# Sixty-four bytes of padding that move the split weight pieces against the token tiles

## The chip, the cores and the metric

One core of a Trainium2 chip. The metric is the device time of the slowest core in microseconds (us); with one core it is that core's. Three runs of the kernel before were timed, and one more execution was recorded by the hardware profiler.

## The reference

Two layers of a hybrid decoder, on 256 tokens of width 1024. In each layer:

```
h = rms_norm(x, ln_w)
q, k, v, g, z, xbc, dt = split(h @ w_in)
attn = moba_attention(rms_norm(q), rms_norm(k), v) * silu(g)
y    = rms_norm(ssd_scan(silu(conv(xbc)), softplus(dt)) * silu(z))
x    = x + concat(attn, y) @ w_out
```

Everything is float32. By far the most arithmetic is in the two projections, `h @ w_in` (1024 by 6672) and the product with `w_out` (2048 by 1024). The scan needs a running sum of `dt * a` over the 256 tokens for each of 16 heads.

## The kernel before

**How a float32 product is made.** The large products are matmuls on the type float32r. A copy into that type rounds, so each operand is split in two: the rounded value, a high piece, and the rest, a low piece. Tokens are split into `hT` and `lT` (in the first stage `hr` and `lr`, in the output projection `ah`/`al` and `sh`/`sl`), weights into `wh` and `wl`. A product is three matmuls: high by high, token low by weight high, token high by weight low.

**How weights come in.** `Weights.pump` (L88) loads pieces of 128 partitions by 2 by 512 floats into one of four `raw` buffers (L76, a DMA issued by SP, L79), makes `wh` from it on ScalarE (L101) and `wl` on VectorE (L102). There are eight `wh` and eight `wl` buffers, of 4096 bytes per partition each, and the pieces are made as far ahead as those allow.

**The two loops that use them.** Both take a weight piece after the other, in the order of the list CHUNKS.

- `mm_tokens` (L212, matmuls at L226 to L228) makes v, q, k and the output projection. The stationary operand is a 128 by 128 block of tokens and the moving one a weight piece, 512 columns wide (348 or 344 for v, and 256 for the last output block).
- `mm_pair` (L233, matmuls at L244 to L246) makes the convolution input, the gates g and z. Here the stationary operand is a 128 by 128 block of a weight piece, and the moving one is 256 tokens.

```
pe.matmul(ps[:, cs], lh[:, kl, tl], wh[:, kk, cs], ...)   # L226, mm_tokens: stationary, moving
pe.matmul(o, wh[:, kk, cs], lh[:, k, :], ...)             # L244, mm_pair: stationary, moving
```

Each matmul brings a weight load of its own (LDWEIGHTS, the engine row PEld), which reads the stationary operand from SBUF while the matmul ahead of it still streams its moving operand.

**What sets the order.** The order of work on TensorE is the order of the program with small tasks (transposes, attention heads, the scan) put in after a set count of steps (`resume`, `tick`). None of it depends on addresses.

**Where the tiles lie.** Pools take SBUF one after the other: `const`, `keep`, `tmp`, `small`, `raw_pool`, `wh_pool`, `wl_pool` (L126 to L132). All token tiles are in `keep`: `hT` begins at byte 38016 of each partition, `lT` at 46208, `ah` at 54400, `al` at 62592, `sh` at 78976, `sl` at 87168. Each of these is 128 more than a multiple of 256. The eight `wh` buffers begin at 162752 and the eight `wl` at 195520, 4096 bytes apart, each 192 more than a multiple of 256, and the `raw` buffers from 146368, 192 more as well. Blocks inside these tiles begin at multiples of 512 bytes. So wherever a token block and a weight piece meet in TensorE, their starts differ by 64 bytes modulo 256: the moving weight is 64 ahead in `mm_tokens`, the moving tokens are 64 behind in `mm_pair`.

`cT` (L417, in `decay`) is a tile of the pool `small`: 16 partitions by 256 floats, 1024 bytes, at byte 144544, with a single buffer. VectorE copies the running sums into it, a DMA stores it to DRAM (L420), and two transposes read it (L427). Behind it in memory come only the last tiles of `small` and then `raw`, `wh` and `wl`, which end at 228288 of 229376 bytes.

Of the kernel before, what the change touches and what calls it, by code (L numbers as in the profile page):

```python
# [9 lines left out]
F32 = mybir.dt.float32  # L10
# [6 lines left out]
S = 256  # L17
# [4 lines left out]
NS = 16  # L22
# [26 lines left out]
class Weights:  # L49
# [38 lines left out]
    def pump(self, upto=None, before=None):  # L88
        nc = self.nc
        upto = len(self.subs) if upto is None else upto  # L90
        while self.prepped < upto and self.prepped - self.freed < NB:
            i = self.prepped
            li, s, wd = self.subs[i]
            self.load(li + RAWB - 1)
            src = self.raw[li]
# [18 lines left out]


RAWB = 4
WARM = 14
URGENT = 400

# [2 lines left out]
def hybrid_kernel(ctx: ExitStack, tc: tile.TileContext, x, par, w, out):  # L122
# [6 lines left out]
    small = ctx.enter_context(tc.tile_pool(name="small", bufs=4))  # L129
    raw_pool = ctx.enter_context(tc.tile_pool(name="raw_pool", bufs=RAWB))  # L130
    wh_pool = ctx.enter_context(tc.tile_pool(name="wh_pool", bufs=NB))
# [5 lines left out]
    def bank(name):  # L137
        return ps_s.tile([P, 512], F32, tag="ps_s", name=name)
# [24 lines left out]

    for i in range(WARM):
        pe.matmul(warm[:, 0:P], ones, ones, start=(i == 0), stop=(i == WARM - 1))

# [223 lines left out]
    def decay(L, dtr, dt, dth, ac, nac, cb):  # L390

        pc = L * NPAR

        def sm_tile(name):
            return small.tile([P, 2, NS], F32, tag=name, name=name, bufs=1)
        ab, e1, zd, z2, pl, da = (sm_tile(n) for n in ("ab", "e1", "zd", "z2", "pl", "da"))
        act.activation(ab, dtr, AF.Abs)
        act.activation(e1, ab, AF.Exp, scale=-1.0)
        dve.tensor_scalar(zd, e1, 2.0, None, ALU.add)
        dve.reciprocal(zd, zd)  # L400
        dve.tensor_tensor(zd, zd, e1, ALU.mult)
        dve.tensor_tensor(z2, zd, zd, ALU.mult)
        dve.tensor_scalar(pl, z2, 1.0 / 17.0, None, ALU.mult)
        for i in range(7, 0, -1):
            dve.scalar_tensor_tensor(pl, pl, 1.0 / (2 * i + 1), z2, ALU.add, ALU.mult)
        dve.scalar_tensor_tensor(pl, pl, 1.0, zd, ALU.add, ALU.mult)
        dve.tensor_scalar(pl, pl, 2.0, None, ALU.mult)
        dve.scalar_tensor_tensor(dt, dtr, 0.0, pl, ALU.max, ALU.add)
        ea = small.tile([P, NS], F32, tag="ea", name="ea", bufs=1)
        act.activation(ea, par_sb[:, pc + C_AL:pc + C_AL + NS], AF.Exp)  # L410
        dve.tensor_tensor(da, dt, ea.unsqueeze(1).to_broadcast([P, 2, NS]), ALU.mult)
        dve.tensor_scalar(dth, dt, 0.5, None, ALU.mult)
        yield 6
        cp = bank("cp")
        pe.matmul(cp[:NS, 0:256], da[:, 0, :], tri[:, 128:384], start=True, stop=False)
        pe.matmul(cp[:NS, 128:256], da[:, 1, :], tri[:, 128:256], start=False, stop=True)
        cT = small.tile([NS, S], F32, tag="cT", name="cT", bufs=1)  # L417
        dve.tensor_copy(cT, cp[:NS, 0:256])
        cd = dram.tile([NS * S], F32, tag="cd", name=f"cd{L}")
        nc.sync.dma_start(cd.rearrange("(h s) -> h s", h=NS), cT)  # L420
        for g in range(NG):
            src = cd[g * 8 * S:(g + 1) * 8 * S].unsqueeze(0).broadcast_to([P, 8 * S])
            nc.sync.dma_start(cb[g].rearrange("p h s -> p (h s)"), src)
        yield 1
        cq = bank("cq")
        for t in range(2):
            pe.transpose(cq[:, t * NS:(t + 1) * NS], cT[:, t * P:(t + 1) * P], ident[:NS, :NS])  # L427
        dve.tensor_copy(ac, cq[:, 0:NS])
        dve.tensor_scalar(nac, cq[:, NS:2 * NS], -1.0, None, ALU.mult)
# [118 lines left out]
    for L in range(NL):  # L548
# [53 lines left out]
        for cs, ts in (((0,), (0, 1)), ((1,), (0, 1)), ((2,), (0, 1))) if L == 0 else (  # L602
# [8 lines left out]
            if L > 0 and ts == (0,):  # L611
                region.__exit__(None, None, None)
        resume(decay(L, dtr, dt, dth, ac, nac, cb))
        qT = keep.tile([P, NH, S], F32, tag="qT", name=f"qT{L}")
        kT = keep.tile([P, NH, S], F32, tag="kT", name=f"kT{L}")
# [153 lines left out]
```

## Time and profile before

| | |
|---|---|
| median of 3 runs | 453.44 us (453.14 to 454.38) |
| profiled execution | 452.3 us |
| its span on the core | 450.5 us |
| TensorE matmul busy | 446.1 us (99%) |
| weight loads busy | 406.0 us (90%) |
| VectorE busy | 346.7 us (77%) |
| ScalarE busy | 279.7 us (62%) |
| granted TensorE clock | 1.00 of 2.4 GHz |

The span is the time from the first to the last instruction of the profiled execution; 1.8 us of its own time lie outside it. Busy time of TensorE counts from a matmul's start to its modelled end, and matmuls overlap; the step from the start of one matmul to the start of the next is what tells how fast TensorE goes.

### The profile page before, as it was taken

Reading aid. Unit: us, or ns where it says so; the run is one execution under the profiler, and the core shown is the slowest. Engines: PE = TensorE matmul, PEld = TensorE weight load, DVE = VectorE, ACT = ScalarE, POOL = GpSimd, SP = SyncE. Lnnn points to the kernel's source line nnn. Section 1 sums busy time; section 2 is a strip of 40 time slices with the busy share of each in tenths; the row PEclk is TensorE's granted clock in tenths of the full one; section 3 lists DMA queues with packets and bytes.
Section 4 is the critical chain, followed back from the end, with each engine's and each line's share of the span. In section 5 each row is a group of like instructions: output and inputs, shape, how many; then the busy total and the mean of one; then the engine's idle time right before and its main releaser. Section 6 shows DMA issues by size and latency. Waiting matters only on the chain.

```text
span 450.5 us, 7880 instructions
## 1 busy us (share of the span) xinstructions
PE 446.1 (99%) x2956; PEld 406.0 (90%) x2956; DVE 346.7 (77%) x636; ACT 279.7 (62%) x571; POOL 23.9 (5%) x29
## 2 busy tenths in 40 slices
PE   9999999999999999999999999999999999999997
PEld 9998878999999999888899878889999989998986
DVE  7597876799999888766565784686999999787621
ACT  7776779778558645534556656977657865555400
POOL 0000320200000000000000011110000000000000
PEclk9999999999999999999999999999999999999999
DMA  8888886452355155556246988561435444553301
GB/s 282 275 250 294 284 302 249 143 185 95 95 188 176 60 160 186 169 188 182 61 138 232 284 278 288 185 227 53 139 109 175 139 141 128 200 180 121 121 25 70
DMA packets 26373, 79.43 MB, mean 176 GB/s; under 512 B 2624, under 2 KB 9440, under 8 KB 25824
## 3 DMA queue, kind: packets, MB, share of 16 engines
q1 hardware_dynamic: 26048, 78.68, 53.3%
q8 instruction: 23, 0.38, 0.3%
q10 hardware_dynamic: 288, 0.27, 0.2%
q14 instruction: 14, 0.11, 0.1%
HBM read 77.85 MB, written 1.08 MB: 175 GB/s over the span
## 4 chain that ended last, share of the span: by engine, by line
PE 99%; DVE 0%; issue 0%
PE o L227 6%; PE o L226 6%; PE o L228 6%; PE xb L244 5%; PE xb L246 5%; PE xb L245 5%; PE z L245 3%; PE v L228 3%; PE z L244 3%; PE v L226 3%; PE v L227 3%; PE z L246 3%; PE k L227 3%; PE g L246 3%; PE g L244 3%; PE g L245 3%
## 5 line engine op out<-in xcount | busy, mean ns | idle before, releaser
L102 DVE TENSOR_TENSOR wl<-raw,wh 128x1024 fp32r<-128x1024 f32 (+3 forms) x145 | 166.0, 1157 | 41.3 <-ACT wh L101 40.1
L101 ACT CAST wh<-raw 128x1024 fp32r<-128x1024 f32 (+3 forms) x145 | 143.9, 999 | 59.8 <-DMA raw<-in_w_dram 15.9
L244 PE MATMUL xb<-hT,wh 128*128 128x256 f32 x192 | 56.3, 293 | 0.0
L245 PE MATMUL xb<-lT,wh 128*128 128x256 f32 x192 | 54.4, 283 | 0.0
L246 PE MATMUL xb<-hT,wl 128*128 128x256 f32 x192 | 53.9, 281 | 0.0
L245 PEld LDWEIGHTS xb<-lT,wh 128*128 128x128 f32 x192 | 36.2, 189 | 0.3
L246 PEld LDWEIGHTS xb<-hT,wl 128*128 128x128 f32 x192 | 36.2, 189 | 0.1
L244 PEld LDWEIGHTS xb<-hT,wh 128*128 128x128 f32 x192 | 36.2, 188 | 0.2
L246 PE MATMUL g<-hT,wl 128*128 128x256 f32 x128 | 36.3, 283 | 0.0
L245 PE MATMUL z<-lT,wh 128*128 128x256 f32 x128 | 36.2, 283 | 0.0
L244 PE MATMUL g<-hT,wh 128*128 128x256 f32 x128 | 36.1, 282 | 0.0
L244 PE MATMUL z<-hT,wh 128*128 128x256 f32 x128 | 36.0, 281 | 0.0
L245 PE MATMUL g<-lT,wh 128*128 128x256 f32 x128 | 35.9, 281 | 0.0
L246 PE MATMUL z<-hT,wl 128*128 128x256 f32 x128 | 35.9, 280 | 0.0
L447 DVE SCALAR_TENSOR_TENSOR cv<-rw,par_sb,cv 128x256 f32<-128x256 f32 x72 | 31.6, 481 | 4.2 <-ACT cv L444 4.2
L226 PE MATMUL k<-wh,hT 128*128 128x512 f32 x64 | 25.4, 397 | 0.0
L227 PE MATMUL k<-wh,lT 128*128 128x512 f32 x64 | 25.4, 397 | 0.0
L228 PE MATMUL k<-wl,hT 128*128 128x512 f32 x64 | 25.4, 397 | 0.0
L227 PE MATMUL q<-wh,lT 128*128 128x512 f32 x64 | 25.1, 394 | 0.0
L226 PE MATMUL q<-wh,hT 128*128 128x512 f32 x64 | 25.1, 394 | 0.0
L227 PE MATMUL o<-wh,al 128*128 128x512 f32 (+1 forms) x64 | 24.7, 386 | 0.0
L228 PE MATMUL q<-wl,hT 128*128 128x512 f32 x64 | 24.6, 395 | 0.0
(197 smaller groups left out, 1106.6 us busy)
## 6 DMA issues: line engine op xcount, KB each, us to landing
raw<-in_w_dram SPq DMA_DIRECT2D x120, 512.0 KB, 4.3
raw<-in_w_dram SPq DMA_DIRECT2D x15, 348.0 KB, 3.7
cb<-cd SPq DMA_DIRECT2D x4, 1024.0 KB, 7.8
raw<-in_w_dram SPq DMA_DIRECT2D x8, 344.0 KB, 3.6
x<-in_x_dram SPq DMA_DIRECT2D x2, 512.0 KB, 5.2
xT<-in_w_dram SPq DMA_DIRECT2D x3, 256.0 KB, 4.3
out_dram<-x SPq DMA_DIRECT2D x3, 256.0 KB, 2.0
raw<-in_w_dram SPq DMA_DIRECT2D x2, 174.0 KB, 3.2
```

Source lines behind the costliest of these rows:

```text
L101: nc.scalar.copy(h[:, ks, :wd], src[:, ks, :wd])
L102: nc.vector.tensor_tensor(lo[:, ks, :wd], src[:, ks, :wd], h[:, ks, :wd].bitcast(F32), ALU.subtract)
L226: pe.matmul(ps[:, cs], lh[:, kl, tl], wh[:, kk, cs], start=first, stop=False)
L227: pe.matmul(ps[:, cs], ll[:, kl, tl], wh[:, kk, cs], start=False, stop=False)
L228: pe.matmul(ps[:, cs], lh[:, kl, tl], wl[:, kk, cs], start=False, stop=final)
L244: pe.matmul(o, wh[:, kk, cs], lh[:, k, :], start=(k == 0 and c == 0), stop=False)
L245: pe.matmul(o, wh[:, kk, cs], ll[:, k, :], start=False, stop=False)
L246: pe.matmul(o, wl[:, kk, cs], lh[:, k, :], start=False, stop=(k == KT - 1 and c == 1))
L447: dve.scalar_tensor_tensor(cv[:, c, :], rw[:, c, k:k + S], cw(k), cv[:, c, :], ALU.mult, ALU.add)
```

## The change

The tile `cT` gets 16 more floats in each partition, and only its first 256 are used. Every tile that lies behind it moves up by 64 bytes: the `raw`, `wh` and `wl` buffers now begin at multiples of 256, and so 128 bytes away from the token tiles, modulo 256, instead of 64. No instruction is added, removed or moved.

```diff
 RAWB = 4
+CT_PAD = 16
 WARM = 14
 URGENT = 400
...
-        cT = small.tile([NS, S], F32, tag="cT", name="cT", bufs=1)
+        cT = small.tile([NS, S + CT_PAD], F32, tag="cT", name="cT", bufs=1)[:, :S]
         dve.tensor_copy(cT, cp[:NS, 0:256])
```

## Rows read from the trace of the kernel before

**Rows 1.** The page: busy time of each engine, then the granted clock by slices.
```profile
PE 446.1 (99%) x2956; PEld 406.0 (90%) x2956; DVE 346.7 (77%) x636; ACT 279.7 (62%) x571; POOL 23.9 (5%) x29
...
PEclk9999999999999999999999999999999999999999
```

**Rows 2.** The page: the chain that ended last, shares of the span by engine.
```profile
PE 99%; DVE 0%; issue 0%
```

**Rows 3.** Waits of the weight loads: who waited for whom, us in total, times, longest.
```profile
PEld warm L165 <- DVE ones L159: 1.1, 1, 1.1
...
PEld cq L427 <- DVE wl L102: 0.7, 2, 0.4
...
PEld q L226 <- ACT wh L101: 0.2, 1, 0.2
```

**Rows 4.** Groups of PE by line and form: operands, count, busy us, mean ns.
```profile
L244 PE MATMUL xb<-hT,wh 128*128 128x256 f32 x192 | 56.3, 293 | 0.0
...
L244 PE MATMUL z<-hT,wh 128*128 128x256 f32 x128 | 36.0, 281 | 0.0
...
L226 PE MATMUL q<-wh,hT 128*128 128x512 f32 x64 | 25.1, 394 | 0.0
...
L226 PE MATMUL o<-wh,ah 128*128 128x512 f32 x56 | 22.1, 395 | 0.0
...
L226 PE MATMUL v<-wh,hT 128*128 128x348 f32 x32 | 10.2, 324 | 0.0
```

**Rows 5.** Timeline of PE, mm_pair: first and last of 50 matmuls, start us.
```profile
153.38 0.28 PE L244 MATMUL g<-hT,wh 128*128 128x256 f32 x1
...
158.93 0.28 PE L245 MATMUL z<-lT,wh 128*128 128x256 f32 x1
```

**Rows 6.** The same later: first and last of 135 matmuls.
```profile
162.09 0.28 PE L246 MATMUL z<-hT,wl 128*128 128x256 f32 x1
...
177.87 0.28 PE L245 MATMUL z<-lT,wh 128*128 128x256 f32 x1
```

**Rows 7.** Timeline of PE, mm_tokens, 512 columns: first and last of 105 matmuls.
```profile
33.10 0.39 PE L226 MATMUL q<-wh,hT 128*128 128x512 f32 x1
...
56.90 0.39 PE L228 MATMUL q<-wl,hT 128*128 128x512 f32 x1
```

**Rows 8.** The same in the second layer: first and last of 62 matmuls.
```profile
252.69 0.40 PE L228 MATMUL q<-wl,hT 128*128 128x512 f32 x1
...
266.92 0.40 PE L226 MATMUL k<-wh,hT 128*128 128x512 f32 x1
```

**Rows 9.** Timeline of PE, mm_tokens, 348 columns: first and last of 71 matmuls.
```profile
8.15 0.32 PE L227 MATMUL v<-wh,lr 128*128 128x348 f32 x1
...
19.35 0.32 PE L226 MATMUL v<-wh,hr 128*128 128x348 f32 x1
```

**Rows 10.** Timeline of PE: seven float32 transposes of 128 columns, two float32 matmuls of 256.
```profile
87.33 0.93 PE L354 MATMUL qtp<-ident,qn 128*128 128x128 f32 x7
...
105.17 0.59 PE L456 MATMUL bp<-bc 128*128 128x256 f32 x2
```

**Rows 11.** Groups of PE by line: the same transposes and matmuls, with their means.
```profile
L354 PE MATMUL qtp<-ident,qn 128*128 128x128 f32 x64 | 8.7, 274 | 0.0
...
L456 PE MATMUL bp<-bc 128*128 128x256 f32 x8 | 2.4, 377 | 0.0
```

**Rows 12.** Timeline of all engines in mm_pair: matmul and weight load side by side.
```profile
153.72 0.28 PE L244 MATMUL g<-hT,wh 128*128 128x256 f32 x1
153.72 0.19 PEld L245 LDWEIGHTS g<-lT,wh 128*128 128x128 f32 x1
```

**Rows 13.** Busy time of VectorE in three windows: window, length, busy us (instructions).
```profile
107.00:120.00 13.00, 13.00 (x27) 1.00 0.48 143
133.00:147.00 14.00, 14.00 (x30) 1.00 0.46 149
325.00:340.00 15.00, 15.00 (x31) 1.00 0.39 125
```

## The prediction

> **What bounds the kernel.** The page first: TensorE's matmuls are busy for 99% of the span, at the full clock (1.00, 2.4 GHz) in every slice [rows 1]. The chain that ended last says the same: 99% of it is PE, none is an engine that PE waited for [rows 2]. The waits of the weight loads name no wait above 1.1 us, and that one is the start of the kernel [rows 3]. So the end is set by TensorE's own pace: by the step from the start of one matmul to the start of the next, times their number.
>
> The groups by form give the numbers [rows 4]. `mm_pair` has (192 + 128 + 128) x 3 = 1344 matmuls of 256 columns (xb, g and z; three lines each). `mm_tokens` has 720 of 512 columns (q and k 64 each, o 56 each of two kinds, three lines each: 192 + 192 + 336), 288 of 348 or 344 (v), and 96 of 256, in all 1104. The mean ns in those rows hold each matmul's run out of the array and overlap, so I read steps from the timeline, as the distance from a first to a last row over their count.
>
> - `mm_pair`: 49 steps in 5.55 us, 113.3 ns [rows 5]; later 134 steps in 15.78 us, 117.8 ns [rows 6].
> - `mm_tokens`, 512 columns: 104 steps in 23.80 us, 228.9 ns [rows 7]; later 61 in 14.23 us, 233.3 ns [rows 8]. For 348 columns: 70 in 11.20 us, 160.0 ns [rows 9].
>
> The same work thus has two steady paces, each held without change for dozens of matmuls while VectorE, ScalarE and the DMAs do quite different things beside it. Counting all undisturbed steps of `mm_pair`, 423 are near 113 and 814 near 118; of those with 512 columns about one in six is in the slower pace.
>
> What would the pace be with nothing in its way? The float32 transposes and matmuls take two cycles a column. Seven transposes of 128 columns take 0.93 us with a last one of 0.274, so the step is (0.93 - 0.274)/6 = 0.109 us for 256 cycles; two matmuls of 256 columns step by 0.59 - 0.377 = 0.213 us for 512 cycles [rows 10, 11]; I take 0.215, between that and twice 0.109. They have weight loads too, but read the moving operand at half the rate. So 256 cycles can go by in 109 ns and 512 in 215. Against that the split products pay 4 to 9 ns a matmul at 256 columns, 14 to 18 at 512, and about 12 at 348 (160 against 148 by proportion). Three of the steady paces are whole multiples of 6.67 ns, which is 16 columns or 64 bytes of the moving operand: 113.3 is 17, 160.0 is 24, 233.3 is 35. Something makes TensorE wait in units of 64 bytes of SBUF, in a pattern that does not depend on other engines. The weight load that starts together with each matmul [rows 12] reads SBUF at that time, and its start is 64 bytes away from the moving operand's, modulo 256. That is the distance which the change turns into 128.
>
> **The change part by part.** No instruction, DMA or wait is added, removed or moved, on any queue, SP's and POOL's included. Three things shift.
>
> 1. *The steps of the split products.* The trace has only distance 64 for them, so the effect has bounds alone. From below: all the excess over the float32 pace goes, 720 x 15 = 10.8 us (230 against 215), 288 x 12 = 3.5, 96 x 9 = 0.9, 1344 x 7.3 = 9.8 (116.3 against 109, from the two counts), in all 25.0 us. From above I reason from the steps: a whole 6.67 ns more on each of the 1104 weight-moving matmuls is +7.4 us, which is half of what they pay now. Zero lies between. During one weight load the moving operand covers about twice the bytes (256 columns, 1024 bytes, beside 128 columns, 512 bytes), so their distance runs through 512 bytes, twice through 256. The 512-column matmuls pay 15/6.67 = 2.2 units, as if each turn cost one. From 64 away one of the meetings falls near an end of the load, where the next one begins; from 128 away both fall a quarter from the ends. I take it that this spares one unit in the weight-moving matmuls, 1104 x 6.67 = 7.4 us, and lets `mm_pair` stay in the quicker pace that it already shows, 1344 x (116.3 - 113.3) = 4.0 us. The nearest rows for that are the quicker paces themselves [rows 5, 7]. Sum: -11.4 us.
>
> By the Trainium skill ("TensorE: Matmul & The Clock Gate", part 2, step by step) the moving operand and the weight load have independent SBUF read ports, so that loading the next weights takes nothing from the running matmul; by that, step 1 is worth 0. The trace does not bear it out for these products (14 to 18 ns over the pace of two-cycle columns), but it does not show either that the weight load is the cause.
>
> 2. *VectorE, ScalarE and the DMAs* read and write `raw`, `wh` and `wl` at shifted addresses, all three by the same 64 bytes. I take 0 for it: what hides it is the eight buffers made ahead, and weight loads wait for L101 and L102 0.2 and 0.7 us in all [rows 3]. The cover is thinnest where VectorE has no idle time at all, in 42 us of the convolution stage [rows 13]. Were everything on VectorE slower there by a tenth, at most 4 us would show.
>
> 3. *What is late next.* In those same 42 us a TensorE that goes 2.5% faster asks for pieces 1 us earlier, and VectorE cannot give them; up to 1 us of the gain may come back as waits for `wl`. I leave that in the range.
>
> The profiled execution took 452.3 us, so the sum gives 440.9; it stands 1.1 under the median of the runs shown, 453.44, and on that the forecast is 442.0.
>
> **Rivals.**
>
> *A, nothing changes.* The extra nanoseconds belong to the float32r stream itself (its rate, or the writes to PSUM) or depend on the distance in no way that a shift by 64 bytes alters: two meetings per load at any distance. For it: the meetings are two from 64 as from 128. Against it: two paces of the same instruction at the same addresses show that how the streams lie in time counts, and so should how they lie in space. 453.4 us. The independent ports of the Trainium skill's page say the same, and that is part of this chance.
>
> *B, slower.* The place is the same weight load beside the moving operand. If after a meeting the waiting stream falls in behind the other, a start at 128 can bring a third meeting into the load where 64 gave two and a bit. Price: one unit on the 1104 weight-moving matmuls, +7.4 us, 460.8; or, milder, every matmul in its slower pace, 423 x 4.5 + 590 x 4.4 = 4.5 us, 457.9. It decides as soon as more than about a third of the matmuls settle in a slower pace than now. For it: both steady paces exist, and `mm_pair` is mostly in its slower one at a distance that someone might call just as good. Against it: nothing but the symmetry of 128.
>
> *C, much faster.* The excess goes almost wholly, -20 to -25 us, 430 us. It needs that 128 keeps the two streams apart for the whole load, which their unequal rates speak against.
>
> *D, the padding does not do what it says.* If the tile were given its room in a way that the 64 bytes vanish, nothing would move; the sizes in `small` and the room behind `wl` (1088 bytes) speak against it. Within A.
>
> **How the numbers follow.** Forecast, faster by about 11 us or a part of it: 0.49. C: 0.08. A with D: 0.19. B: 0.24. The forecast's own range goes from 434 (most of step 1's 25 us on one kind of loop) to 449.5 (only `mm_pair` gains, -4.0 us). The whole range takes in A and the milder B and ends at 459; below 434 lies most of C and above 459 the full B, together less than 2 in 10. About 0.3%, 1.4 us, is what a measurement of this kernel can tell from no change. Faster by more than that 0.57, within it 0.19, slower 0.24.
>
> **What would show it.** Step 1 is right if the 512-column steps fall to about 222 ns and those of 348 to about 153, each by one unit, and `mm_pair` runs at 113.3 throughout. A rival A shows unchanged steps, B steps of 235 to 240 ns or 118 and more everywhere. Step 2 is wrong if weight loads wait for L101 or L102 by several us. Point 3 shows as waits for `wl` between 107 and 147 us. The forecast is wrong if the steps do not change, or if they do and the number of distinct paces and not their floor has changed.

## The result and the profile after

The kernel with the padding took 457.85 us (457.69 to 458.06, 4 runs) against 453.29 us (452.51 to 454.38, 4 runs) before: a ratio of 1.0105 [1.0085, 1.0124]. It is slower by 4.6 us, where 11.4 us of gain were forecast.

The profiled execution of after took 458.06 us, that of before 452.3. Its page, with the three lines that answer to [rows 1, 2]:

```profile
PE 450.9 (99%) x2956; PEld 408.8 (90%) x2956; DVE 347.2 (76%) x636; ACT 279.6 (61%) x571; POOL 24.8 (5%) x29
...
PEclk9999999999999999999999999999999999999999
...
PE 94%; DMA 2%; DVE 1%; ACT 1%; SPq 1%; issue 0%; POOL 0%
```

The counts are the same as before, the clock is full in every slice, and TensorE is still busy for 99%. Its busy time is 4.8 us longer for the same 2956 matmuls, so time went into the matmuls and not between them. The waits of the weight loads, answering to [rows 3], say the same:

```profile
PEld warm L166 <- DVE ones L160: 1.1, 1, 1.1
...
PEld rg L322 <- DVE dg L317: 1.0, 1, 1.0
PEld cq L428 <- DVE wl L102: 0.7, 2, 0.4
PEld v L229 <- DVE wl L102: 0.4, 1, 0.4
```

(Lines behind L117 are one higher than before.) On its way back the chain leaves TensorE at two of these waits, for `wl` (0.4 us, at 25.8 us) and for `dg` (1.0 us, at 20.6 us), and so its shares of the other engines are work of the first 26 us. No wait is long enough to carry 4.6 us. The groups of matmuls by form [rows 4] are dearer by 2 to 4 ns a matmul:

```profile
L245 PE MATMUL xb<-hT,wh 128*128 128x256 f32 x192 | 56.8, 296 | 0.0
...
L245 PE MATMUL z<-hT,wh 128*128 128x256 f32 x128 | 36.2, 283 | 0.0
...
L227 PE MATMUL q<-wh,hT 128*128 128x512 f32 x64 | 25.3, 398 | 0.0
```

These means hold the run out of the array, so, as in the prediction, the steps tell more. From the timeline of TensorE, first and last matmul of four undisturbed stretches: `mm_tokens` with 348 columns, 512 columns, `mm_pair`, and 512 columns in the second layer:

```profile
7.80 0.32 PE L227 MATMUL v<-wh,hr 128*128 128x348 f32 x1
...
19.16 0.32 PE L229 MATMUL v<-wl,hr 128*128 128x348 f32 x1
...
33.30 0.39 PE L228 MATMUL q<-wh,lT 128*128 128x512 f32 x1
...
58.73 0.40 PE L229 MATMUL q<-wl,hT 128*128 128x512 f32 x1
...
164.66 0.28 PE L246 MATMUL z<-lT,wh 128*128 128x256 f32 x1
...
181.27 0.28 PE L245 MATMUL z<-hT,wh 128*128 128x256 f32 x1
...
255.57 0.39 PE L227 MATMUL q<-wh,hT 128*128 128x512 f32 x1
...
270.67 0.40 PE L229 MATMUL k<-wl,hT 128*128 128x512 f32 x1
```

- 348 columns: 71 steps in 11.36 us, 160.0 ns, as in [rows 9].
- 512 columns: 109 steps in 25.43 us, 233.3 ns, where the same q stage took 228.9 [rows 7]; later 65 steps in 15.10 us, 232.3, where it took 233.3 [rows 8].
- `mm_pair`: 140 steps in 16.61 us, 118.6 ns, where the same z stage took 117.8 [rows 6]. It keeps about 118.6 in most stretches and 120.0 in some short ones, most of them in the second layer; the pace of 113.3 [rows 5] does not occur in any long stretch.

Added up over the whole trace, step by step, the two profiled executions differ by 5.76 us from the first to the last start of a matmul: `mm_pair` took 165.67 us instead of 162.47 (+3.20), the 512-column matmuls 169.47 instead of 167.69 (+1.78), those of 344 columns +0.38, of 348 +0.10, of 256 in the last output block +0.06, and everything else on TensorE +0.24. So nearly all of it is the pace of the two loops: mean undisturbed steps of 118.76 and 232.52 ns where they were 116.27 and 229.90. Their +5.0 us is what to set beside the 4.6 us of the medians. The rest varies from one execution to the next: the kernel with a whole 256 bytes of padding, below, has the old paces, and its profiled execution took 2.0 us more between the same two starts than that of before.

### The profile page after: what moved, and what is told of

It is laid out like the page before. It is cut to its first block, busy times and chain, and to the rows that moved or that the text cites. A ratio compares the mean times of both kernels' runs of the same rounds, so it can differ in the third digit from the quotient of the medians.

```text
span 456.3 us, 7880 instructions
## 1 busy us (share of the span) xinstructions
PE 450.9 (99%) x2956; PEld 408.8 (90%) x2956; DVE 347.2 (76%) x636; ACT 279.6 (61%) x571; POOL 24.8 (5%) x29
## 4 chain that ended last, share of the span: by engine, by line
PE 94%; DMA 2%; DVE 1%; ACT 1%; SPq 1%; issue 0%; POOL 0%
PE o L228 6%; PE o L227 6%; PE o L229 6%; PE xb L247 5%; PE xb L246 5%; PE xb L245 5%; PE z L246 3%; PE z L245 3%; PE g L247 3%; PE g L246 3%; PE z L247 3%; PE g L245 3%; PE q L227 3%; PE k L227 3%; PE k L228 3%; PE q L229 3%
## 5 line engine op out<-in xcount | busy, mean ns | idle before, releaser
L102 DVE TENSOR_TENSOR wl<-raw,wh 128x1024 fp32r<-128x1024 f32 (+3 forms) x145 | 165.9, 1155 | 43.9 <-ACT wh L101 42.8
L101 ACT CAST wh<-raw 128x1024 fp32r<-128x1024 f32 (+3 forms) x145 | 143.6, 1000 | 64.1 <-DMA raw<-in_w_dram 19.8
L186 POOL TENSOR_TENSOR rr<-se,mhalf 128x4 f32<-128x4 f32 x16 | 19.0, 1190 | 117.9 <-DVE se L345 117.9
```

Of the source, the lines that this page charges most:

```text
L101: nc.scalar.copy(h[:, ks, :wd], src[:, ks, :wd])
L102: nc.vector.tensor_tensor(lo[:, ks, :wd], src[:, ks, :wd], h[:, ks, :wd].bitcast(F32), ALU.subtract)
L186: pool.tensor_tensor(o, i, mhalf[:, :n], ALU.pow)
```

## The experiments

The theory after the result: the pace hangs on the start of the moving operand against that of the stationary one, modulo 256 bytes. Below, **distance** is the moving operand's start less the stationary one's, modulo 256. Weights move in `mm_tokens` and stand in `mm_pair`, so the two loops have opposite distances: 64 and 192 before, 128 and 128 after. Rivals: the weight buffers' own place modulo 256; any move of the layout; `raw`, and with it the DMAs, ScalarE and VectorE; other work beside the matmuls.

**A whole 256 bytes.**

```diff
-CT_PAD = 16
+CT_PAD = 64
```

> Padding of 64 floats instead of 16: raw, wh and wl move by 256 bytes, so that the distance to the token tiles is 64 modulo 256 as in the kernel before. Theory 1 (the pace hangs on the distance of the weight pieces from the token tiles modulo 256): as before, 453.3 us within 1.4, steps of 113.3 and 117.8 ns for mm_pair and of 228.9 and 233.3 for 512 columns. Rival 2 (it hangs on where the weight buffers themselves begin modulo 256): the same 453.3. Rival 3 (the distance counts in whole bytes, or any move away from the old place costs): 456 to 459.

453.11 us against 453.13, ratio 1.0 [0.9989, 1.0011]; mean steps 116.26 and 229.89 ns. The buffers lie elsewhere, and the old paces are back, so a move as such costs nothing; only its remainder modulo 256 counts.

**Tokens and weights moved together.** The kernel before, with 64 bytes ahead of both:

```diff
-    table = const.tile([P, 1], F32, name="table")
+    table = const.tile([P, 17], F32, name="table")[:, :1]
```

> No padding of cT; instead 64 bytes of padding in the pool const, ahead of the token tiles, so that token tiles and weight buffers move up by 64 bytes together: the weight buffers begin at multiples of 256 as in the kernel after, the distance to the token tiles stays 64. Theory 1 (distance): as before, 453.3 within 1.4. Rival 2 (the weight buffers' own place): as after, 457.9 within 1.4, with steps of 118.7 for mm_pair and 232.4 for 512 columns.

452.88 us, 0.9995 [0.9984, 1.0007]; 116.26 and 229.50 ns. The weight buffers lie at multiples of 256 here, as in the slower kernel, and nothing is lost. The rival that their own place decides falls.

**The other two distances.**

```diff
-CT_PAD = 16
+CT_PAD = 32
```

> Padding of 32 floats: the weight buffers begin 64 bytes behind the token tiles modulo 256, where they were 64 ahead. Theory 1: the two loops swap roles (moving operand 64 ahead in mm_pair, 64 behind in mm_tokens); a pace of its own, not that of before: the 256-column matmuls of the output projection, which had the moving operand 64 ahead, show 117.8 before, so mm_pair should now be at 117.8 throughout (+2 us), and mm_tokens at steps not seen yet. Rival 2: also a place not seen yet, 450 to 460. The run tells whether either kernel can be beaten by the same means.

```diff
-CT_PAD = 16
+CT_PAD = 48
```

> Padding of 48 floats: weight buffers and token tiles begin at the same place modulo 256. Theory 1: if equal starts collide most, the slowest of the four distances, 459 to 465; if two streams that start together and part at once collide least, the fastest, under 452. Rival 2: no forecast, 450 to 460.

456.01 us, 1.0064 [1.0047, 1.008], and 456.13 us, 1.0062 [1.0045, 1.008]. Neither came out as expected: 48 floats gave neither the slowest nor the fastest of the four, and with 32 `mm_pair` was not at 117.8 throughout. They take nearly the same time, out of opposite parts. The timeline of TensorE for 48 floats (distance 0 in both loops), first and last of a stretch of each loop:

```profile
33.23 0.40 PE L228 MATMUL q<-wh,lT 128*128 128x512 f32 x1
...
57.94 0.39 PE L229 MATMUL q<-wl,hT 128*128 128x512 f32 x1
...
164.24 0.28 PE L247 MATMUL z<-hT,wl 128*128 128x256 f32 x1
...
180.92 0.28 PE L245 MATMUL z<-hT,wh 128*128 128x256 f32 x1
```

109 steps of 226.7 ns, the quickest yet, and 139 steps of 120.0, the slowest. And for 32 floats (distance 192 in `mm_tokens`, 64 in `mm_pair`), with a stretch of `mm_pair` in each layer:

```profile
33.34 0.39 PE L228 MATMUL q<-wh,lT 128*128 128x512 f32 x1
...
58.54 0.39 PE L228 MATMUL q<-wh,lT 128*128 128x512 f32 x1
...
120.02 0.28 PE L245 MATMUL xb<-hT,wh 128*128 128x256 f32 x1
...
128.03 0.28 PE L247 MATMUL g<-hT,wl 128*128 128x256 f32 x1
...
385.04 0.28 PE L247 MATMUL z<-hT,wl 128*128 128x256 f32 x1
...
401.93 0.28 PE L246 MATMUL z<-lT,wh 128*128 128x256 f32 x1
```

108 steps of 233.3 ns; 68 of 117.8 and 149 of 113.4. The mean steps are 117.01 and 233.32 ns for 32 floats, 119.70 and 227.69 for 48 (`mm_pair`, then 512 columns). The two loops want different distances, and of the four shifts that of before has the least sum.

**`raw` alone moved.** The changed kernel, with 192 bytes ahead of `wh`; only `raw` keeps its new place:

```diff
+    fill = wh_pool.tile([P, 48], F32, tag="fill", name="fill", bufs=1)
+    dve.memset(fill, 0.0)
```

> The padding of the change (16 floats behind cT), and 48 more floats between the raw buffers and the wh buffers: raw begins at a multiple of 256 as in the kernel after, wh and wl begin 64 ahead of the token tiles as in the kernel before. Theory 1 (matmul and weight load, distance of wh and wl from the token tiles): as before, 453.2 within 1.4. Rival 4 (the shifted DMA writes, or the reads of raw by ScalarE and VectorE, slow something down): as after, 457.9.

453.66 us against 453.17, 1.0004 [0.9989, 1.0019]. What ScalarE, VectorE and the DMAs do at the shifted `raw` costs nothing.

**The matmuls alone, at sixteen distances.** The kernel before, with a block of float32r matmuls on tiles of ones ahead of it, while TensorE has nothing else to do. Up to about 40 us VectorE and ScalarE still split the first weights and tokens beside it; from then on until the block ends no other engine is busy:

```
for d in range(16):                      # 4 floats, 16 bytes a step; letters a to p
    for i in range(24):
        pe.matmul(ps[:, 0:n], st[:, k:k + 128], mv[:, 4 * d:4 * d + n], ...)
```

> The kernel before with a block ahead of it: two float32r tiles filled with ones, matmuls of one kind alone (24 in a row, twice, with a float32 matmul between), stationary blocks at a fixed place modulo 256, the moving operand 0, 16, 32 .. 240 bytes away, for 512, 348 and 256 columns; then 512 columns with stationary blocks of 128, 64 and 32 columns at the distances 0, 64 and 128. No other engine has work to do with it. Theory 1: the steps repeat the paces of the four kernels at the same distances: 512 columns 226.7 at 0, 228.9 or 233.3 at 64, 232.4 at 128, 233.3 at 192; 256 columns 120.0 at 0, 117.8 at 64, 118.7 at 128, 113.3 or 117.8 at 192; and with narrower stationary blocks, whose loads read less, the steps of 512 columns fall towards 215. Rival A (the float32r stream's own rate): with narrower blocks the steps stay at 227 to 233, and the distance of the starts makes no difference here. Rival 5 (work of the other engines takes part): other paces than in the kernels.

The timeline of TensorE inside blocks at distance 0, 64, 128 and 192 (letters a, e, i, m), for 512 columns (w) and 256 (h); for 512 columns at distance 0 a later series (`sax`), since the first ran before 40 us. A row is a run of matmuls: start, length, and the count at the end; the step is the length less that of the last matmul (0.39 or 0.28), over one less than the count:

```profile
54.82 3.60 PE L194 MATMUL we<-mv,st 128*128 128x512 f32 x15
...
100.83 3.65 PE L194 MATMUL wi<-mv,st 128*128 128x512 f32 x15
...
147.34 3.43 PE L194 MATMUL wm<-mv,st 128*128 128x512 f32 x14
...
322.26 2.32 PE L194 MATMUL ha<-mv,st 128*128 128x256 f32 x18
...
346.68 2.28 PE L194 MATMUL he<-mv,st 128*128 128x256 f32 x18
...
371.14 2.33 PE L194 MATMUL hi<-mv,st 128*128 128x256 f32 x18
...
395.68 2.32 PE L194 MATMUL hm<-mv,st 128*128 128x256 f32 x19
...
421.18 3.56 PE L203 MATMUL sax<-mv,st 128*128 128x512 f32 x15
```

So (3.56 - 0.39)/14 = 226.4 ns at distance 0, and from the w rows 229.3, 232.9 and 233.8 (a row is good to half a nanosecond or so); 120.0, 117.6, 120.6 and 113.3 for 256 columns. Beside the kernels, with the start of every matmul read singly once a series has settled:

| distance | 512 columns alone | in a kernel | 256 columns alone | in a kernel |
|---|---|---|---|---|
| 0 | 226.6 | 226.7 (48 floats) | 120.0 | 120.0 (48 floats) |
| 64 | 228.9 | 228.9, 233.3 (before) | 117.8 | 117.8, 113.3 (32 floats) |
| 128 | 232.4 | 233.3, 232.3 (after) | 120.0, 118.7 | 120.0, 118.6 (after) |
| 192 | 233.3 | 233.3 (32 floats) | 113.3, 117.7 | 113.3, 117.8 (before) |

The kernels' paces come back with no other engine at work, and the last rival falls. The other twelve distances give nothing lower than 226.6 ns (at 112) and 113.3 ns (also at 112). The narrower stationary blocks of this run did not fall towards 215, as was expected: 228.1 to 231.2 ns with 64 columns, 230.9 to 231.8 with 32. And two series of the same matmuls at the same addresses can settle apart: at distance 48 the first went at 233.2 ns, the second at 230.1.

**Both loops at distance 112.** This was built from the sweep. `wh` and `wl` get spare room and start inside it, and to make that room the kernel keeps 3 `raw` buffers instead of 4:

```diff
-RAWB = 4
-CT_PAD = 16
+RAWB = 3
+OFF_T, OFF_P = 28, 36
+CT_PAD = 48
...
+            h = self.wh_pool.tile([P, 1088], F32R, tag="wh", name=f"wh{i}")
+            h = h[:, o:o + 1024].rearrange("p (k n) -> p k n", k=KS)
```

> Each loop gets the distance at which the sweep was quickest. The wh and wl buffers get 256 bytes more each (three raw buffers instead of four make the room), and a piece is written 112 bytes ahead of the token tiles modulo 256 when mm_tokens will use it, 112 behind when mm_pair will, so that the moving operand begins 112 bytes ahead of the stationary one in both. Theory 1: 512 columns step by 226.7 ns instead of 229.9, 720 x 3.2 = 2.3 us less; mm_pair by 113.3 instead of 116.3, 1344 x 3.0 = 4.0 less; the 256-column blocks of the output 0.4 less, v 0.1 more: 453.2 - 6.6 = 446.6, if the third raw buffer less costs nothing. Rival (the sweep's paces hold for ones and for equal operands alone, or supply takes the gain back): 452 or more.

(`CT_PAD = 48` puts the buffers at distance 0; `OFF_T` and `OFF_P` add to it in floats, for the two loops.) The same with distances 64 and 192, as before, to take out what the lost buffer costs:

```diff
-OFF_T, OFF_P = 28, 36
+OFF_T, OFF_P = 16, 16
```

> The same kernel with three raw buffers and the longer wh and wl buffers, but every piece written 64 bytes ahead of the token tiles, as in the kernel before. If the room and the third raw buffer cost nothing: 453.2 within 1.4, with the old steps. If three raw buffers are too few: above 455, with waits for DMA ahead of L101 and of weight loads.

466.35 us, 1.0307 [1.0281, 1.0333], and 461.69 us, 1.02 [1.0178, 1.0221], against 452.85. The gain did not come, and of the control's two cases the dear one holds. The lost buffer costs 8.8 us: ScalarE's waits for `raw` in the control and, below, in the kernel before (us in total, times, longest):

```profile
ACT wh L103 <- DMA raw<-in_w_dram: 57.5, 49, 3.3
```

```profile
ACT wh L101 <- DMA raw<-in_w_dram: 15.9, 24, 1.6
```

And distance 112 is worse than the control by 4.7 us, not better: `mm_pair` has a mean step of 119.57 ns where the control has 116.02, and 1344 x 3.55 ns is 4.8 us. Two stretches of `mm_tokens` and one of `mm_pair`, from its timeline of TensorE:

```profile
35.43 0.39 PE L232 MATMUL q<-wl,hT 128*128 128x512 f32 x1
...
50.91 0.40 PE L230 MATMUL k<-wh,hT 128*128 128x512 f32 x1
...
59.93 0.39 PE L230 MATMUL q<-wh,hT 128*128 128x512 f32 x1
...
67.86 0.40 PE L232 MATMUL q<-wl,hT 128*128 128x512 f32 x1
...
169.55 0.28 PE L248 MATMUL z<-hT,wh 128*128 128x256 f32 x1
...
188.99 0.28 PE L248 MATMUL z<-hT,wh 128*128 128x256 f32 x1
```

67 steps of 231.0 ns, then 35 of 226.6 at the same addresses modulo 256, and 162 of 120.0. One distance has several steady paces, and the one that a bare loop settled in need not be the kernel's.

**How much is the weight load's.** Again a block ahead of the kernel before: stationary blocks of 128, 64, 32 and 16 columns (their loads took 188, 134, 109 and 95 ns), which make the output narrower by as much, and one of bfloat16, at several distances.

> The kernel before with a block ahead of it, as in the sweep: float32r matmuls of 512 and 256 columns whose stationary block has 128, 64, 32 or 16 columns, at the distances 0, 64, 112 and 128 bytes, and bfloat16 ones with 128. The output of the kernel is unchanged. If the whole excess over 215 (109) ns came from the weight load's reads, 16 columns would step by about 215 (109) at every distance. If the float32r stream itself pays most of it and the load only shifts it, 16 columns step by 228 to 233 (113 to 120) with no dependence on the distance. bfloat16 moves half the bytes a column: by the first it would still pay something and depend on the distance, by the second 215 and 109 without any dependence.

The timeline inside 512-column blocks: float32r with 128 stationary columns at distance 0 and 128, with 16 at the same two, and bfloat16 at 0; then bfloat16 with 256 columns at distance 0:

```profile
8.48 3.57 PE L196 MATMUL rwax<-mv,st 128*128 128x512 f32 x15
...
41.96 3.42 PE L196 MATMUL rwau<-mv,st 128*128 128x512 f32 x14
...
145.58 3.64 PE L196 MATMUL rwdx<-mv,st 128*16 128x512 f32 x15
...
180.27 3.63 PE L196 MATMUL rwdu<-mv,st 128*16 128x512 f32 x15
...
197.34 3.62 PE L196 MATMUL bwax<-mb,sb 128*128 128x512 bf16 x16
...
322.62 2.13 PE L196 MATMUL bhax<-mb,sb 128*128 128x256 bf16 x18
```

By the same working: 227.1 and 233.1 ns with the full load, 232.1 and 231.4 with one an eighth as wide, 215.3 in bfloat16; 108.8 for 256 columns in bfloat16, against 120.0 in float32r. (Read singly, the settled starts give 226.7 and 232.4, then 230.9 to 231.7, and 215.9; 109.2 and 120.0.) So the stationary block has a part in it, by its load or by the output that narrows with it, which this run does not part: take most of it away and the spread over distances 0, 64 and 128 shrinks from 5.7 ns to under one. But the pace does not fall towards 215 then. It settles at 231, slower than with the full load at distance 0. Nor does the narrow load end the several paces: with 16 stationary columns distance 112 still had two, 228.9 and 235.5, and 256 columns still ran at 113.3 or at 120. In bfloat16, where both operands have half the bytes, the excess and its dependence are gone (215.8 to 215.9 and 109.1 to 109.2 at 0, 64 and 128). That block loads all 128 stationary columns, and writes the same float32 output as the float32r one. Its loads and those of 16 float32r columns (count, busy us, mean ns):

```profile
L196 PEld LDWEIGHTS <-sb 128*128 128x128 bf16 x288 | 28.2, 98 | 17.2
...
L196 PEld LDWEIGHTS rwdx<-mv,st 128*16 128x16 f32 x48 | 4.6, 95 | 6.0
```

The two loads take about the same time, 98 and 95 ns, and the matmuls step by 215.9 and 231 ns. So neither the length of the load nor the writes to PSUM alone can explain the excess. What is left is what float32r operands take themselves, as they are read or in the array; the runs do not part these.

**Each loop at its better distance of the four.** Four `raw` buffers again, the room found in a tile (`bc`) that now shares another's place; q, k and the output projection at distance 0, the rest as before:

```diff
-CT_PAD = 16
+CT_PAD = 48
+OFF_T, OFF_P = 0, 16
...
+ self.subs.append((len(self.loads), s, wd, OFF_T if name[0] in "qko" else OFF_P))
...
-        bc = keep.tile([P, 4, S], F32, tag="bc", name=f"bc{L}")
+        bc = tmp.tile([P, 4, S], F32, tag="sq", name=f"bc{L}", bufs=1)
```

> Four raw buffers again; the room for 256 more bytes in each wh and wl buffer comes from bc, which now shares a buffer with the squares of the norm (tag sq). The pieces for q, k and the output projection are written at the same place modulo 256 as the token tiles (distance 0, 226.7 ns a step in the kernel with 48 floats of padding, in one pace alone), the others 64 ahead as in the kernel before. Theory 1: 720 matmuls of 512 columns at 226.9 instead of 229.9 give -2.1 us at most (the padding kernel's total was 1.6 under that of before), the 256-column output blocks +0.2, mm_pair and v as before: 451.3 to 451.9 us, against the control. Rival (a pace measured in one kernel does not carry over, as with the 112 bytes): 452.5 to 456.

And with all of it at the distances of before:

```diff
-OFF_T, OFF_P = 0, 16
+OFF_T, OFF_P = 16, 16
```

> The same layout with every piece 64 ahead of the token tiles, as in the kernel before. If the shared buffer and the longer buffers cost nothing: 453.0 within 1.

451.93 us (450.77 to 454.31, 12 runs) against 452.7, 0.9972 [0.9957, 0.9988], and the control 452.66, 0.9994 [0.9981, 1.0007]. From the timeline of TensorE in the first:

```profile
33.75 0.40 PE L232 MATMUL q<-wl,hT 128*128 128x512 f32 x1
...
57.78 0.39 PE L230 MATMUL q<-wh,hT 128*128 128x512 f32 x1
...
83.16 0.28 PE L249 MATMUL xb<-lT,wh 128*128 128x256 f32 x1
...
87.92 0.28 PE L249 MATMUL xb<-lT,wh 128*128 128x256 f32 x1
```

106 steps of 226.7 ns, and 42 of 113.3. The 512-column matmuls have a mean step of 227.72 ns where they had 229.90, and 720 x 2.2 ns is 1.6 us; 0.8 came out, just beyond the slow end of what was expected. The interval against the kernel before reaches to within 0.12% of no change. Its own control, which has the same layout, is 0.7 us slower, but the runs of the two overlap (450.77 to 454.31 and 451.85 to 453.84), so this gain is at the edge of what can be told. The profiled execution is the slowest of the twelve, and it has a wait that the control's has not (us in total, times, longest):

```profile
PE pp L384 <- DVE sc L379: 1.7, 1, 1.7
```

It eats what the steps give in that execution; whether the quicker ones have it is not known.

## Why the prediction was wrong

**What bounds the kernel** held: TensorE's pace, step by step, with no wait of note before or after. So did the place: the distance between a moving and a stationary operand modulo 256 is what the change acts through, and no other effect of it was found.

**Step 1** failed, and with it the sign. It said that "from 128 away both fall a quarter from the ends", and that "this spares one unit in the weight-moving matmuls" and "lets `mm_pair` stay in the quicker pace", -11.4 us. Measured, the 512-column step went from 229.90 to 232.52 ns, that of 348 columns stayed at 160.0 in the stretch of [rows 9], and `mm_pair` went from 116.27 to 118.76: +1.78, +0.10 and +3.20 us. Three things were wrong in it.

- *Where the excess comes from.* The step put the 14 to 18 ns over 215 down to meetings with the weight load, by their number. The runs with a narrow load refute that: with an eighth of the load the step is 231 ns, and not near 215, while bfloat16, with a load just as short, steps by 215.9. Some 11 ns (226.6 against 215.8) stayed at every distance and with every load that was tried, and what the distance moves is the rest, from 226.6 to 236.6 ns over the sixteen. With that, the lower bound of 25 us was out of reach as well: 720 x 11 alone is 7.9 us of it.
- *The unit.* It counted in whole units of 6.67 ns, which fit three of the five paces it read. The other two, 117.8 ns for most of `mm_pair` and 228.9 for most steps of 512 columns, are 17.7 and 34.3 units, and 118.6 and 232.3 ns, found after the change, are 17.8 and 34.8. "Spares one unit" had no step to come from.
- *Which distance is good.* The argument from the symmetry of 128 had no row behind it; the trace had one distance only for each loop, and from that the paces of others do not follow. At 128 each loop is at the second slowest of its four. Nor is there a best one for both: `mm_tokens` is quickest at 0, where `mm_pair` is slowest.

The Trainium skill ("TensorE: Matmul & The Clock Gate", part 2, step by step) has two independent read ports, so that a weight load takes nothing from the running matmul, and a back-to-back gap of N/2.4 + about 2.5 ns, by which 512 columns would take an estimated 215.8 ns and 256 columns 109.2. The blocks in bfloat16 agree to the tenth, at every distance tried. The float32r blocks do not, by 11 to 21 ns at 512 columns, and there the measurement decides.

**Step 2** held: weight loads wait 0.2 us for L101 and 1.1 for L102 in the longest rows, with `raw` alone moved the time is 1.0004 of before, and with `raw`, `wh` and `wl` at the new places and the tokens moved too it is 0.9995. **Point 3**, VectorE late for a quicker TensorE, was not tested by this change, since TensorE got slower: where VectorE had no idle time in three windows [rows 13], it now has some in two of them.

```profile
107.00:120.00 13.00, 13.00 (x26) 1.00 0.34 112
133.00:147.00 14.00, 13.74 (x31) 1.00 0.35 116
325.00:340.00 15.00, 13.55 (x29) 1.00 0.19 60
```

**The rivals.** B came true in its milder form, "every matmul in its slower pace", 457.9 us, where 457.85 was measured. The size is partly luck: it gave 1.9 us to `mm_pair` and 2.6 to 512 columns, and it was 3.2 and 1.8, because `mm_pair` found paces above its slower one (118.6 and 120.0). Its mechanism, a third meeting inside the load, is not shown. A (no change) and C fell with the steps, though A's reason, that the extra nanoseconds belong to the float32r stream itself, fits the 11 ns that nothing removed; its other suspect, the writes to PSUM, does not, since bfloat16 makes the same ones. D fell with the first experiment: the padding does move the pieces. The time lies in the range; the sum had no ground for preferring its sign.

**What stays open** is why a distance has the pace it has, and what makes a run of matmuls settle in one of several. It is not chance from one execution to the next: in the kernels with the distances of before, `mm_pair` took 162.47 us in that of before, 162.46 with a whole 256 bytes and 162.46 with both moved, each stretch in the same pace in all three. Nor is it the distance alone: a stretch of 71 steps of 512 columns in the second layer went at 233.3 ns before and at 228.9 with both moved. The phase in which a loop starts would be a candidate; it was not tried.

## What to carry to other kernels

Where float32r matmuls set the time, the start of one operand's tile against the other's, modulo 256 bytes, was worth a per cent here, and the paces seen give no rule for it: measure each loop, in the kernel itself, at the few shifts that the layout allows. A tile that grows by 64 bytes far away shifts everything behind it, so when a change with no other cause moves the time by a per cent, look at the steps of the matmuls and at the starts of their tiles, and pad back by a whole 256 bytes to see whether it goes away. Room for such padding must not come out of a buffer that hides the DMA: that cost 8.8 us here, and the best placing gave 0.8, hardly more than the runs scatter.

## What the runs showed of the hardware

- TensorE's steps in float32r lock into flat or short repeating patterns and stay there for a hundred matmuls and more, many of them whole units of 6.67 ns (113.3 is 17, 120.0 is 18, 160.0 is 24, 226.7 is 34, 233.3 is 35), some of them not (117.8, 118.7, 232.3).
- One distance can have more than one: 113.3 and 117.8 ns with the same operands in the same kernel, 226.7 and 231.0 at distance 112. Which one a stretch of `mm_pair` takes was the same in three kernels with the same distances.
- A full stationary block beside the stream can make it quicker than a narrow one: 226.7 ns with 128 columns against 231 to 232 with 16 at distance 0.
- bfloat16 shows nothing of this: 215.8 and 109.2 ns at distances 0, 64 and 128, with full weight loads of 98 ns, where those of float32r took 188.
